# Value products in groups of four, two and two head pairs; the first layer's values in the transposes' banks; more time counted for the heads' transfers

## The chip, the cores and the metric

One core of a Trainium2 chip runs the whole program in one launch. The metric is device time in microseconds (us) of one execution. Of the kernel before, three runs took 275.78, 276.76 and 276.71 us (median 276.71). A fourth execution, the profiled one, took 275.99 us, of which 274.2 us lie between its first and its last instruction; the 1.8 us around that span stand in no row.

## What is computed

A small decoder of two layers over 256 tokens of width 1024, all in float32 accuracy:

```
h = x @ w_in;  c_q, c_kv, k_rope, gate = split(h)          # layer A, latent attention
q  = rms_norm(c_q) @ w_uq;   k_nope, v = rms_norm(c_kv) @ w_ukv
s  = (q_nope . k_nope + q_rope . k_rope) * scale, causal;  p = softmax(s);  o = p @ v
x1 = LayerNorm(alpha * x + (o * silu(gate)) @ w_o)
...
k, v = split(x1 @ w_kv);  q, gate = split(x1 @ w_in)       # layer B, 256 tokens are one block
o  = softmax(causal(rope(q) . rope(k)) * scale) @ v
out = LayerNorm(alpha * x1 + (o * silu(gate)) @ w_o)
```

Both layers have 16 heads with values of 64 columns; the kernel treats them as eight pairs.

## The kernel before

**Products.** TensorE (PE) works on float32r operands. Each factor is split into a high part and a rest (`wh`/`wl` for weights, `act_h`/`act_l`, `x_h`/`x_l`, `big_h`/`big_l` for activations), by `split` (line 400 on ScalarE, line 411 or 415 on VectorE or GpSimd), and each product is three passes: high by high, high by rest, rest by high (`passes`). All are recorded by one helper, so they share line 430; transposes have line 444.

**Order.** No engine's order is written by hand. Every operation is recorded as an `Op` with a counted duration, and `Schedule.order` simulates five queues (PE, ACT, DVE, POOL, SP) with these counts, keeps account of buffers, and writes one fixed order for each engine. At run time each engine works through its own list strictly in order and waits on semaphores. A transfer is counted as landed 1300 ns after its share of the DMA queue, plus `late`, which only the first weights had so far (`LATE`).

```
            if e == "sp":
                x = max(t + 1100, dma)
                dma = x + o.size / 330.0
                o.end = dma + 1300 + o.late
```

**PSUM.** Eight banks: two `s` (scores), two `pt` (transposes), one `pv` (value products), three `proj` (everything else); see `PSUM_BUFS`.

**Attention** (`attention`, both layers). For each pair: `scores` on PE, the softmax on DVE and ACT (tile `e`), fill-in products (`fill`: keys, queries and gates of later pairs), then `transp` (three transposes of `e` per head, copied out to tile `pt`). After every second pair `values` multiplies the transposed weights with the value tile `V`: 64 output columns per head, so two heads share the array, side by side. DVE then multiplies each pair's result by its gate `G` (tile `oa`), and `split` makes `big_h` and `big_l`, the operands of the output product. So each layer has four calls of `values`, of two pairs each, all in the one `pv` bank.

**Heads of layer B.** `rope_moba` makes rotated queries and keys in tile `x_h`; `move_heads` brings them into the heads' layout (tiles `kq0`, `kq1` and `x_l`) by 64 transfers on the SP queue.

**Layer A's values** (`token_products("uv", ...)`) fill four banks, two per half of the tokens ("token 0" and "token 1" below, 128 tokens each), all from the three `proj` banks.

**End.** The last `token_products("ob", ...)` multiplies `big_h`/`big_l` with the output weights: token 0 in two `proj` banks, token 1 in two `s` banks (columns 0 to 511, then 512 to 769) and a `proj` bank (768 to 1023). The seventh and eighth weight units lie in `x_h`/`x_l`, so those products read `x_h,big_h`, `x_l,big_h`, `x_h,big_l`; they need the last two pairs' `big` tiles. `finish_b` does token 0's layer norm on DVE (tile `m`); `last_b` does token 1's in pieces; both end in transfers to `out`.

Of the kernel before, what the change touches and what calls it, by code (L numbers as in the profile page):

```python
# [13 lines left out]
P = 128  # L14
D = 1024
S = 256
# [10 lines left out]
GATES_FIRST = 2  # L27
RAW_BUFS = 5
HL_BUFS = 6
G_BUFS = 5  # L30
LAG = 8
PSUM_BUFS = {"s": 2, "pt": 2, "pv": 1, "proj": 3}

# [20 lines left out]
PLAIN = 2  # L54
PIECES = 4
LATE = 2000

LANES = 8


def on(*key):
    return "pool" if key in POOL else "dve"
# [76 lines left out]
def A(x):  # L139
    if isinstance(x, View):  # L140
        return x.ap()
    return x.tile() if isinstance(x, Val) else x
# [225 lines left out]
def trunk(ctx, tc, W0, xtok, W, WO, gq, gkv, lng, lnb, cosa, sina, coska, sinka, cosb, sinb, maskd, identd, out):  # L368
    nc = tc.nc
# [8 lines left out]
    def C(shape, tag, dtype=F32, at=0):  # L378
        return sc.val(cp, shape, dtype, tag, at=at)

    def T(shape, tag, bufs=2, dtype=F32):
        return sc.val(tp, shape, dtype, tag, bufs)

    def bank(tag):
        return sc.val(pp, [P, 512], F32, tag, PSUM_BUFS[tag])
# [5 lines left out]
    def dma(o, i, size, part=False, r=None, late=0):  # L391
        sc.op("sp", 650 if part else 525, lambda: nc.sync.dma_start(A(o), A(i)), [i] if r is None else r, [o], size).late = late

    def act(o, i, n, func=AF.Copy, scale=1.0, bias=0.0, accum=None):
        dur = (n + (61 if is_ps(i) else 112)) / 1.2
        dur += 93 * (accum is not None) + 93 * isinstance(scale, (View, Val)) + 93 * isinstance(bias, (View, Val))

        def go():
            if func is AF.Copy:
                nc.scalar.copy(A(o), A(i))  # L400
            elif accum is None:
                nc.scalar.activation(A(o), A(i), func, bias=A(bias), scale=A(scale))
            else:
                nc.scalar.activation(A(o), A(i), func, bias=A(bias), scale=A(scale), accum_out=A(accum))  # L404

        sc.op("act", dur, go, [i, scale, bias], [o] + ([accum] if accum is not None else []))
# [20 lines left out]
    def mms(calls, o, r, dur):  # L427
        def go():
            for (out_, lt, rh, st, sp_) in calls:
                nc.tensor.matmul(A(out_), A(lt), A(rh), start=st, stop=sp_, skip_group_check=True)  # L430

        sc.op("pe", dur, go, r, o if isinstance(o, list) else [o], k=len(calls))
# [4 lines left out]
    def passes(o, ah, al, bh, bl, start, stop, n, r=None):  # L437
        mms([(o, ah, bh, start, False), (o, ah, bl, False, False), (o, al, bh, False, stop)],
            o, [ah, al, bh, bl], 3 * mm_cost(n))
# [8 lines left out]
    def split(h, l, src, n, scale=None, eng="dve"):  # L448
        if scale is None:
            act(h, src, n)  # L450
            tt(l, src, h.f32(), ALU.subtract, n, eng)
        else:
            act(h, src, n, AF.Identity, scale=scale)
            stt(l, src, scale, h.f32(), ALU.mult, ALU.subtract, n)
# [10 lines left out]
    def load_raw():  # L465
# [3 lines left out]
        if u < 8:  # L469

            for c0, c1 in ((0, 512), (512, 1280)) if u < PLAIN else ((0, 1280),):
                dma(r[:, c0:c1].at(c0), W0[u, :, c0:c1], (c1 - c0) * 512, late=LATE * (u > 0))
            split(xh[:, u, :].at(u), xl[:, u, :].at(u), r[:, 0:S].at(0), S)
# [49 lines left out]
    def wsl(w, c0, c1):  # L523
        h, l, kk, early = w
        if early == "ob":
            if c0 == 512 and c1 == 1024:
                return tuple(t.halves() for t in (h, l))
            c0, c1 = (LAST, WOB) if c0 == 768 else (c0, c1)
            return h[:, c0:c1], l[:, c0:c1]
        key = (kk, c0 // S * S if early else 0)  # L530
        return h[:, c0:c1].at(key + (0,)), l[:, c0:c1].at(key + (1,))
# [30 lines left out]
    def token_products(name, nk, lhs, tags, lag, done, last=None, last_residual=None):  # L562
        banks = [None, None]
        n1 = nk * (3 if last else 1)
        for i in range(max(nk, n1 + lag)):
            for tok in range(2):
                j = i - lag * tok
                if not 0 <= j < (n1 if tok else nk):
                    continue
                if j == 0:  # L570
                    banks[tok] = [bank(t) for t in tags[tok]]
                k = j % nk
                w = weights(name, k)
                parts = ((0, 512), (512, 1024))
                if tok and last:
                    parts = (((0, 512), (512, 770), (768, 1024))[j // nk],)
                for c0, c1 in parts:
                    h, l = wsl(w, c0, c1)
                    ah, al = lhs(k, tok)
                    o = banks[tok][j // nk if tok and last else c0 // 512][:, 0:c1 - c0]  # L580
                    if last and c1 - c0 == 512 and c0:
                        o = o.rearrange("p (a b) -> p a b", b=S)
                    if last and tok and c0 == 768 and k == 0:
                        last_residual(o)
                    passes(o, ah, al, h, l, k == 0 and not (last and tok and c0 == 768), k == nk - 1, c1 - c0)
                if tok and last:
                    if k == nk - 1:
                        last(banks[tok][j // nk], c0, c1 // S * S)
                elif j == nk - 1:
                    done(tok, banks[tok])  # L590
# [11 lines left out]
    for k in range(8):  # L602
        w = weights("g1", k)
        a, b = xs(k)
        for c in range(8):
            o = g1[c // 2][:, (c % 2) * S:(c % 2) * S + S]
            if k < PLAIN and c < 2:
                u, v = first_raws[k][:, S + c * P:S + (c + 1) * P].at(0), first_raws[k][:, 0:S].at(0)
# [67 lines left out]
    def gate(name, j, rhs):  # L676
# [3 lines left out]
        act(t, ps[:, :S], S, AF.Tanh, scale=0.5)  # L680
        g = T([P, S], "G", G_BUFS)
        stt(g, t, 1.0, ps[:, :S], ALU.add, ALU.mult, S)
# [35 lines left out]
    for g in range(2):  # L718
        ps = bank("proj")
# [63 lines left out]
    def transp(es):  # L783
        r = []
        for e in es:
            pt = bank("pt")
            transposes(pt, [(pt[:, i * P:(i + 1) * P], e[:, c0:c0 + P]) for i, c0 in enumerate((S, 0, P))], [e])
            t = T([P, 384], "pt", 6)
            act(t, pt[:, :384], 384)
            r.append(t)  # L790
        return r

    def values(la, ps_, pts, Vt, ogh, ogl):

        ps, calls, used = bank("pv"), [], []
        for j, p in enumerate(ps_):
            for t in range(2):
                for s in range(2):
                    v = Vt[:, t, 2 * p + s, :].at((t, (2 * p + s) // 8))
                    calls.append((ps[64 * s:64 * s + 64, j * S + t * P:j * S + S], v, pts[j][s][:, t * S:S + t * P], t == 0, t == 1))  # L800
                    used += [v, pts[j][s]]
        mms(calls, ps, used, 250 + 642 * len(ps_))
        for j, p in enumerate(ps_):
            oa = T([P, S], "oa")
            tt(oa, ps[:, j * S:(j + 1) * S], Gs.pop(p), ALU.mult, S)
            split(ogh[:, p, :].at(p), ogl[:, p, :].at(p), oa, S, eng=on("og", la, p))

    def value_evac(Vt, banks, tok):
        for hf in range(2):
            src = banks[hf].rearrange("p (a b) -> p a b", b=64)  # L810
            act(Vt[:, tok, 8 * hf:8 * hf + 8, :].at((tok, hf)), src, 512)

    def attention(la, heads, fill, scale, Vt, ogh, ogl):
        done = []
        for i in range(8):
            hd, keys = heads(i)
            es = scores(la, i, hd, keys, scale)
            fill(i)
            if len(done) == 2:
                values(la, (i - 2, i - 1), done, Vt, ogh, ogl)  # L820
                done = []
            done.append(transp(es))
        values(la, (6, 7), done, Vt, ogh, ogl)

    def heads_mla(p):
        b = p % 4
# [6 lines left out]
    ogh, ogl = C([P, 8, S], "big_h", F32R, AT_ACT), C([P, 8, S], "big_l", F32R, AT_ACT)  # L833
    kq_mla(0)
    kq_mla(1)
    V = C([P, 2, H, 64], "V")
# [1 line left out]
    def lhs_kv(k, tok):  # L838
        return tuple(t[:, k, tok * P:(tok + 1) * P].at(k) for t in (ch, cl))

    token_products("uv", 2, lhs_kv, (("proj", "proj"), ("proj", "proj")), 2, lambda tok, bk: value_evac(V, bk, tok))

    def fill_a(step):
        for nm, i in PLAN_A[step]:
# [87 lines left out]
    def move_heads(step):  # L932
        while moves and moves[0][0] - 3 <= step:
            p, R, base = moves.pop(0)
            hd = HT[p % 3]
            for s in range(2):
                r0 = base + 32 * s
                for v in range(2):
                    dma(hd[32 * v:32 * v + 32, s, 0:3, :].at((s, v, 0)).f32(), R[r0:r0 + 32, v, 1:4, :].at(None).f32(), 98304, True)
                    dma(hd[64 + 32 * v:96 + 32 * v, s, 0:2, :].at((s, v, 1)).f32(), R[r0:r0 + 32, v, 0:4:2, :].at(None).f32(), 65536, True)  # L940

    def heads_moba(p):
        hd = HT[p % 3]
# [33 lines left out]
    def last_residual(o):  # L977
        mms([(o, idr, rh, True, False), (o, idr, rl, False, False)], o, [idr, rh, rl], 2 * mm_cost(S))
# [132 lines left out]
```

## Time and profile before

| | before |
|---|---|
| median of three runs | 276.71 us (275.78 to 276.76) |
| the profiled execution | 275.99 us, its span 274.2 us |
| TensorE busy | 267.3 us, 97% of the span |
| VectorE busy | 217.0 us, 79% |
| ScalarE busy | 164.1 us, 60% |
| GpSimd busy | 44.8 us, 16% |
| granted TensorE clock, mean | 0.997 |

A busy TensorE row is the time in which some product was on its way; products overlap, so two starts stand closer together than one row is long. Start-to-start distances are the price of a product. Times in the rows count from the first instruction of the span.

### The profile page before, as it was taken

How to read it: one execution, taken by the hardware profiler on the slowest of the kernel's cores; microseconds unless marked ns; L12 is line 12 of the kernel's file. 1: busy time of each engine (PE TensorE's matmuls, PEld its weight loads, DVE VectorE, ACT ScalarE, POOL GpSimd, SP SyncE). 2: the span in 40 equal slices, each digit the busy share in tenths (PEclk: the TensorE clock that was granted, in tenths of full speed). 3: DMA queues.
4: the chain of work that ended last, by engine and by line, in shares of the span. 5: the costliest groups of instructions: out<-in, count | busy, mean ns of one | idle time of the engine just before them, and what ended most of it. 6: DMA issues, size and time to landing. Idle time of an engine off the chain costs nothing.

```text
span 274.2 us, 5384 instructions
## 1 busy us (share of the span) xinstructions
PE 267.3 (97%) x1950; PEld 246.3 (90%) x1950; DVE 217.0 (79%) x494; ACT 164.1 (60%) x366; POOL 44.8 (16%) x46
## 2 busy tenths in 40 slices
PE   8999999999999999999999999999999999999991
PEld 6999999999899988878888899999999999887890
DVE  3776889999998789947997436879978998897584
ACT  4864977477774779914372543637856859986000
POOL 3000162300020021111010000602324214021000
PEclk9999999999999999999999999999999999999998
DMA  7999484777334442470459574466759768440022
GB/s 232 405 400 412 164 278 183 238 266 274 115 118 149 158 155 78 138 247 0 148 175 295 203 255 154 155 187 195 273 128 331 200 220 322 117 127 4 0 78 77
DMA packets 18683, 52.46 MB, mean 191 GB/s; under 512 B 2912, under 2 KB 6112, under 8 KB 18656
## 3 DMA queue, kind: packets, MB, share of 16 engines
q1 hardware_dynamic: 18656, 52.12, 56.4%
q8 instruction: 15, 0.25, 0.4%
q14 instruction: 12, 0.10, 0.1%
HBM read 45.81 MB, written 1.05 MB: 171 GB/s over the span
## 4 chain that ended last, share of the span: by engine, by line
PE 93%; issue 3%; DVE 2%; POOL 0%; POOLq 0%; DVEq 0%
PE proj L430 61%; PE s L430 15%; PE pv L430 8%; PE pt L444 5%; PE pt L430 4%; DVE bst L864 1%; DVE m L415 0%; DVE act_h L415 0%; POOL mv L411 0%; POOLq L1107 0%; DVEq L1107 0%; DVE mv L865 0%; DVE mv L422 0%
## 5 line engine op out<-in xcount | busy, mean ns | idle before, releaser
L411 DVE TENSOR_TENSOR wl<-raw,wh 128x1024 fp32r<-128x1024 f32 (+3 forms) x80 | 85.6, 1090 | 21.3 <-ACT wh L400 21.0
L400 ACT CAST wh<-raw 128x1024 fp32r<-128x1024 f32 (+4 forms) x81 | 73.5, 925 | 36.6 <-PE proj L430 17.8
L430 PE MATMUL proj<-act_h,wh 128*128 128x256 f32 x280 | 79.6, 284 | 0.0
L430 PE MATMUL proj<-act_l,wh 128*128 128x256 f32 x280 | 78.5, 280 | 0.0
L430 PE MATMUL proj<-act_h,wl 128*128 128x256 f32 x280 | 78.5, 280 | 0.0
L430 PEld LDWEIGHTS proj<-act_h,wh 128*128 128x128 f32 x280 | 52.8, 188 | 0.0
L430 PEld LDWEIGHTS proj<-act_l,wh 128*128 128x128 f32 x280 | 52.7, 188 | 0.0
L430 PEld LDWEIGHTS proj<-act_h,wl 128*128 128x128 f32 x280 | 52.7, 188 | 0.0
L404 ACT ACTIVATE e<-e,st 128x256 f32<-128x256 f32 x64 | 28.5, 449 | 6.3 <-DVE st L770 6.2
L411 POOL TENSOR_TENSOR big_l<-oa,big_h 128x256 fp32r<-128x256 f32 x14 | 10.8, 786 | 87.7 <-ACT big_h L400 87.7
L430 PE MATMUL s<-kq 128*128 128x256 f32 (+1 forms) x100 | 19.1, 318 | 0.0
L424 DVE TENSOR_SCALAR e<-e,st 128x256 f32<-128x256 f32 x64 | 18.0, 325 | 0.9
L430 PE MATMUL proj<-x_h,wh 128*128 128x256 f32 x64 | 18.5, 289 | 0.0
L430 PE MATMUL proj<-x_h,wl 128*128 128x256 f32 x64 | 18.0, 281 | 0.0
L430 PE MATMUL proj<-x_l,wh 128*128 128x256 f32 x64 | 18.0, 281 | 0.0
L430 PEld LDWEIGHTS s<-kq 128*128 128x128 f32 x100 | 15.6, 190 | 1.6 <-issue 0.3
L400 ACT COPY pt<-pt 128x384 f32<-128x384 f32 x32 | 14.8, 477 | 1.5 <-PE pt L444 1.3
L411 DVE TENSOR_TENSOR x_l<-raw,x_h 128x256 fp32r<-128x256 f32 (+2 forms) x14 | 10.7, 770 | 5.9 <-ACT x_h L400 5.9
L444 PE MATMUL pt<-ident,e 128*128 128x128 f32 x96 | 15.0, 275 | 0.1
L400 ACT CAST x_h<-raw 128x256 fp32r<-128x256 f32 (+2 forms) x14 | 9.4, 685 | 8.7 <-PE s L430 4.3
L411 POOL TENSOR_TENSOR t<-t,t512b 128x512 f32<-128x512 f32 x5 | 6.8, 1364 | 39.0 <-DVE t L411 21.4
L444 PEld LDWEIGHTS pt<-ident,e 128*128 128x128 f32 x96 | 11.0, 140 | 1.4 <-issue 0.7
(190 smaller groups left out, 570.6 us busy)
## 6 DMA issues: line engine op xcount, KB each, us to landing
raw<-in_W SPq DMA_DIRECT2D x58, 512.0 KB, 4.4
raw<-in_WO SPq DMA_DIRECT2D x8, 528.0 KB, 5.4
raw<-in_W SPq DMA_DIRECT2D x6, 640.0 KB, 6.9
raw<-in_W SPq DMA_DIRECT2D x6, 384.0 KB, 5.9
kq<-x_h SPq DMA_DIRECT2D x24, 96.0 KB, 2.2
kq<-x_h SPq DMA_DIRECT2D x24, 64.0 KB, 2.1
m<-in_xtok SPq DMA_DIRECT2D x2, 512.0 KB, 6.4
lng<-in_lng SPq DMA_DIRECT2D x2, 512.0 KB, 3.6
```

The lines of the kernel that those rows point to most:

```text
L400: nc.scalar.copy(A(o), A(i))
L404: nc.scalar.activation(A(o), A(i), func, bias=A(bias), scale=A(scale), accum_out=A(accum))
L411: sc.op(eng, dur, lambda: e.tensor_tensor(A(o), A(a), A(b), op=op), [a, b], [o], lock=not (is_ps(a) or is_ps(b)))
L424: fn = lambda: e.tensor_scalar(A(o), A(a), A(s1), s2, op0=op0, op1=op1)
L430: nc.tensor.matmul(A(out_), A(lt), A(rh), start=st, stop=sp_, skip_group_check=True)
L444: nc.tensor.transpose(A(x), A(y), A(ident))
L864: sc.op("dve", 600, lambda hf=hf, cs=cs: nc.vector.bn_stats(A(st[:, hf, :]), A(z[:, cs])), [z.at(hf)], [st.at(hf)])
```

## The change

Five edits, one of which (the scratch size, line 1104 of the kernel before) makes room in SBUF for the larger buffers.

- `values` takes up to four pairs; the third and fourth pair go into a second bank, from `proj`. `attention` calls it at pair 4 (pairs 0 to 3), pair 6 (4 and 5) and at the end (6 and 7): three calls a layer. Buffers `G` grow from 5 to 7, `pt` tiles from 6 to 10. The call's counted duration becomes 370 ns plus 642 ns a pair (250 before).
- Layer A's values for token 1 go into the two `pt` banks.
- Each of the 64 transfers of layer B's heads is counted as landing 2000 ns later than before.
- The DMA scratch shrinks to 4096 bytes a partition.

```
-G_BUFS = 5
+G_BUFS = 7
+GROUPS = (4, 6)
+MOVE_LATE = 2000
...
-            t = T([P, 384], "pt", 6)
+            t = T([P, 384], "pt", 10)
...
-        ps, calls, used = bank("pv"), [], []
-        for j, p in enumerate(ps_):
+        banks, calls, used = [bank(t) for t in ("pv", "proj")[:(len(ps_) + 1) // 2]], [], []
+        for i, p in enumerate(ps_):
+            ps, j = banks[i // 2], i % 2
...
-        mms(calls, ps, used, 250 + 642 * len(ps_))
+        mms(calls, banks, used, 370 + 642 * len(ps_))
...
-            if len(done) == 2:
-                values(la, (i - 2, i - 1), done, Vt, ogh, ogl)
+            if i in GROUPS:
+                values(la, range(i - len(done), i), done, Vt, ogh, ogl)
...
-        values(la, (6, 7), done, Vt, ogh, ogl)
+        values(la, range(8 - len(done), 8), done, Vt, ogh, ogl)
...
-    token_products("uv", 2, lhs_kv, (("proj", "proj"), ("proj", "proj")), 2, lambda tok, bk: value_evac(V, bk, tok))
+    token_products("uv", 2, lhs_kv, (("proj", "proj"), ("pt", "pt")), 2, lambda tok, bk: value_evac(V, bk, tok))
...
-                    dma(hd[32 * v:32 * v + 32, s, 0:3, :].at((s, v, 0)).f32(), R[r0:r0 + 32, v, 1:4, :].at(None).f32(), 98304, True)
+                    dma(hd[32 * v:32 * v + 32, s, 0:3, :].at((s, v, 0)).f32(), R[r0:r0 + 32, v, 1:4, :].at(None).f32(), 98304, True, late=MOVE_LATE)
...
-    nc = bacc.Bacc("TRN2", target_bir_lowering=False, num_devices=1)
+    nc = bacc.Bacc("TRN2", target_bir_lowering=False, num_devices=1, dynamic_dma_scratch_size=4096)
```

Since the counts and the groups feed the scheduler, the written orders change in many places. Three of them follow; line 430 of the kernel before is line 434 of the change, and 415 is 419.

PE, layer B, the first value products (`V`) of the kernel before, then those of the change; `pt<-ident,e` are transposes, `s<-` scores.

```order
L430 MATMUL pv<-pt,V 64x256 x2
L430 MATMUL pv<-pt,V 64x128 x2
L430 MATMUL pv<-pt,V 64x256 x2
L430 MATMUL pv<-pt,V 64x128 x2
L444 MATMUL pt<-ident,e 128x128 x3
L430 MATMUL s<-kq_1883 128x256 x2
```

```order
L434 MATMUL s<-kq_1891 128x256 x3
L434 MATMUL pv<-pt,V 64x256 x2
L434 MATMUL pv<-pt,V 64x128 x2
L434 MATMUL pv<-pt,V 64x256 x2
L434 MATMUL pv<-pt,V 64x128 x2
L434 MATMUL proj<-pt,V 64x256 x2
L434 MATMUL proj<-pt,V 64x128 x2
L434 MATMUL proj<-pt,V 64x256 x2
L434 MATMUL proj<-pt,V 64x128 x2
L448 MATMUL pt<-ident,e 128x128 x3
```

Two calls have become one of twice the length, its second half in a `proj` bank; the same stands in layer A.

PE, the end: the last products of token 0 (`proj<-x_h`, `proj<-x_l`) and what follows them, before and in the change. `s<-` are token 1's products.

```order
L430 MATMUL proj<-x_h,big_h 128x512
L430 MATMUL proj<-x_l,big_h 128x512
L430 MATMUL proj<-x_h,big_l 128x512
L430 MATMUL s<-wh,big_h 128x512
L430 MATMUL s<-wl,big_h 128x512
L430 MATMUL s<-wh,big_l 128x512
```

```order
L434 MATMUL proj<-x_h,big_h 128x512
L434 MATMUL proj<-x_l,big_h 128x512
L434 MATMUL proj<-x_h,big_l 128x512
L434 MATMUL s<-x_h,big_h 128x512
L434 MATMUL s<-x_l,big_h 128x512
L434 MATMUL s<-x_h,big_l 128x512
```

Before, 15 products of 512 columns and 15 of 258 columns on the other weight units (`wh`, `wl`) still follow token 0's last one, beside all of those shown as `s<-x_h`; in the change these 30 stand ahead of token 0's last ones. The last call of `values` has moved with them: it stands after 15 of token 1's products, where before it stood ahead of all of them.

DVE, the end: token 0's layer norm (tile `m_293` before, `m_292` in the change) and token 1's (`m_320`); `lng` and `lnb` are the layer norm's factors and offsets.

```order
L864 BN_STATS bst<-m_293 128x6
L865 BN_AGGR mv<-bst 128x2
L422 TENSOR_SCALAR mv<-mv 128x1
L415 SCALAR_TENSOR_TENSOR m_293<-m_293,mv,lng 128x512 x2
L415 SCALAR_TENSOR_TENSOR m_293<-m_293,mv,lnb 128x512 x2
L415 SCALAR_TENSOR_TENSOR m_320<-m_320,s 128x512
```

```order
L419 SCALAR_TENSOR_TENSOR m_292<-m_292,mv,lng 128x512
L419 SCALAR_TENSOR_TENSOR m_320<-m_320,s 128x512
L419 SCALAR_TENSOR_TENSOR ms<-s,ms 128x1
L1002 BN_STATS bst_3397<-m_320 128x6
L419 SCALAR_TENSOR_TENSOR m_292<-m_292,mv,lng 128x512
L419 SCALAR_TENSOR_TENSOR m_292<-m_292,mv,lnb 128x512 x2
```

The instructions are the same ones; in the change token 1's first pieces are interleaved with token 0's, and all of token 0's still stand ahead of token 1's closing statistics (`BN_STATS` of the `proj` bank).

## Rows read from the trace of the kernel before

**Rows 1.** Page, part 1: busy us (share of the span) x instructions.

```profile
PE 267.3 (97%) x1950; PEld 246.3 (90%) x1950; DVE 217.0 (79%) x494; ACT 164.1 (60%) x366; POOL 44.8 (16%) x46
```

**Rows 2.** Waits, PE alone: line waited for, us in total, times, longest.

```profile
PE pv L430 <- PEq L1104: 0.8, 1, 0.8
```

**Rows 3.** Timeline of PE, layer A: start us, us, what (two stretches).

```profile
76.45 0.28 PE L430 MATMUL proj<-act_l,wh 128*128 128x256 f32 x1
76.56 0.28 PE L430 MATMUL proj<-act_h,wl 128*128 128x256 f32 x1
76.90 0.52 PE L444 MATMUL pt<-ident,e 128*128 128x128 f32 x3
...
104.87 0.28 PE L430 MATMUL proj<-x_h,wl 128*128 128x256 f32 x1
105.11 0.67 PE L430 MATMUL s<-kq 128*128 128x256 f32 x2
```

**Rows 4.** Timeline of PE, the end, from token 0's last products.

```profile
254.34 0.40 PE L430 MATMUL proj<-x_h,big_h 128*128 128x512 f32 x1
...
257.14 0.39 PE L430 MATMUL s<-wh,big_h 128*128 128x512 f32 x1
...
262.00 0.28 PE L430 MATMUL s<-wh,big_h 128*128 128x258 f32 x1
...
264.91 0.40 PE L430 MATMUL proj<-act_l 128*128 128x256 f32 x2
...
267.88 0.27 PE L430 MATMUL proj<-x_h,big_l 128*128 128x256 f32 x1
```

**Rows 5.** Timeline of DVE, the end.

```profile
256.63 0.69 DVE L415 SCALAR_TENSOR_TENSOR m<-m,proj 128x512 f32<-128x512 f32 x1 [3.04 <-PE proj L430]
...
262.36 0.68 DVE L415 SCALAR_TENSOR_TENSOR m<-m,s 128x512 f32<-128x512 f32 x1
...
263.74 0.14 DVE L422 TENSOR_SCALAR bst<-bst 128x1 f32<-128x1 f32 x1
265.11 0.42 DVE L415 SCALAR_TENSOR_TENSOR m<-m,s 128x256 f32<-128x256 f32 x1 [1.23 <-PE s L430]
...
266.49 1.27 DVE L415 SCALAR_TENSOR_TENSOR act_h<-m,ms,lng 128x256 f32<-128x256 f32 x3
268.19 0.43 DVE L996 BATCH_NORM_STATS2 bst<-proj 128x6 f32<-128x256 f32 x1 [0.42 <-PE proj L430]
```

**Rows 6.** Timeline of PE around layer B's last value products.

```profile
249.45 0.39 PE L430 MATMUL proj<-wl,big_h 128*128 128x512 f32 x1
249.68 0.39 PE L430 MATMUL proj<-wh,big_l 128*128 128x512 f32 x1
250.00 1.52 PE L430 MATMUL pv<-pt,V 128*64 128x256 f32 x16
251.45 0.50 PE L430 MATMUL proj<-wh,big_h 128*128 128x512 f32 x1
251.79 0.40 PE L430 MATMUL proj<-wl,big_h 128*128 128x512 f32 x1
```

**Rows 7.** Chain that ended last, in order of time: start us, us, what.

```profile
30.67 26.24 PE proj L430 x200
...
72.22 1.31 PE s L430 x8
```

**Rows 8.** DMA view: queues with packets, MB and share; issues with KB and us to landing.

```profile
q1 hardware_dynamic: 18656, 52.12, 56.4%
...
kq<-x_h SPq DMA_DIRECT2D x24, 96.0 KB, 2.2
kq<-x_h SPq DMA_DIRECT2D x24, 64.0 KB, 2.1
```

**Rows 9.** Windows: stretch, length, then busy us (x instructions) of PE, PEld, DVE, ACT, POOL.

```profile
256.63:268.15 11.52, 11.52 (x74) 10.30 (x72) 9.63 (x22) 0.00 (x0) 0.99 (x1) 1.00 0.12 46
```

**Rows 10.** Timeline of DVE and POOL after layer B's last value products.

```profile
251.64 0.76 DVE L411 TENSOR_TENSOR oa<-pv,G 128x256 f32<-128x256 f32 x2
252.58 0.73 POOL L411 TENSOR_TENSOR big_l<-oa,big_h 128x256 fp32r<-128x256 f32 x1 [10.21 <-ACT big_h L400]
252.87 0.72 DVE L411 TENSOR_TENSOR big_l<-oa,big_h 128x256 fp32r<-128x256 f32 x1 [0.47 <-ACT big_h L400]
```

**Rows 11.** Page, part 5: group, count, busy us, mean ns, idle before.

```profile
L411 DVE TENSOR_TENSOR wl<-raw,wh 128x1024 fp32r<-128x1024 f32 (+3 forms) x80 | 85.6, 1090 | 21.3 <-ACT wh L400 21.0
```

More of the change, by code (lines that the diff above doesn't have):

```diff
@@ L799, in values @@
                     v = Vt[:, t, 2 * p + s, :].at((t, (2 * p + s) // 8))
-                    calls.append((ps[64 * s:64 * s + 64, j * S + t * P:j * S + S], v, pts[j][s][:, t * S:S + t * P], t == 0, t == 1))
-                    used += [v, pts[j][s]]
-        mms(calls, ps, used, 250 + 642 * len(ps_))
-        for j, p in enumerate(ps_):
+                    calls.append((ps[64 * s:64 * s + 64, j * S + t * P:j * S + S], v, pts[i][s][:, t * S:S + t * P], t == 0, t == 1))
+                    used += [v, pts[i][s]]
+        mms(calls, banks, used, 370 + 642 * len(ps_))
+        for i, p in enumerate(ps_):
+            ps, j = banks[i // 2], i % 2
             oa = T([P, S], "oa")
@@ L938, in move_heads @@
                 for v in range(2):
-                    dma(hd[32 * v:32 * v + 32, s, 0:3, :].at((s, v, 0)).f32(), R[r0:r0 + 32, v, 1:4, :].at(None).f32(), 98304, True)
-                    dma(hd[64 + 32 * v:96 + 32 * v, s, 0:2, :].at((s, v, 1)).f32(), R[r0:r0 + 32, v, 0:4:2, :].at(None).f32(), 65536, True)
+                    dma(hd[32 * v:32 * v + 32, s, 0:3, :].at((s, v, 0)).f32(), R[r0:r0 + 32, v, 1:4, :].at(None).f32(), 98304, True, late=MOVE_LATE)
+                    dma(hd[64 + 32 * v:96 + 32 * v, s, 0:2, :].at((s, v, 1)).f32(), R[r0:r0 + 32, v, 0:4:2, :].at(None).f32(), 65536, True, late=MOVE_LATE)
     def heads_moba(p):
```

## The prediction

> **What bounds the kernel now.** I read the engine shares first: TensorE is busy for 97% of the span, the next engine for 79% [rows 1]. A busy share could hide waits, so the waits of TensorE alone come second: one, 0.8 us, at the very start [rows 2]. Third, the start-to-start distances of TensorE after the first microseconds: I found two hesitations. One transpose starts 0.34 us after the product ahead of it, where its neighbours stand 0.11 us apart; one score starts after 0.24 us instead of about 0.12 [rows 3]. They are worth 0.23 and 0.12 us, 0.35 us together. So from its start to its last product at 268.15 us (267.88 + 0.27, [rows 4]) TensorE is one unbroken list, and a faster or slower neighbour changes nothing unless TensorE waits for it. Last I read the end: the closing statistics on VectorE start at 268.19, 0.04 us after the last product, and VectorE sat idle for 0.42 us ahead of them [rows 5]. After that start 6.0 us follow (274.2 - 268.19), in which nothing of the change lies. So the time is: the length of TensorE's list, plus what VectorE still has to do when the list ends.
>
> **Part 1: fewer value calls.** Around one call, the start of the last 512-column product ahead (249.68) and that of the second one behind (251.79) lie 2.11 us apart [rows 6]. Two 512-column intervals are 2 x 0.233 = 0.47 us (twelve products from 254.34 to 257.14, [rows 4]). The call's own columns are those of a pair of score calls, which take 1.31 us at full width [rows 7]; here two heads run side by side at half width, so I take 1.31 again, as an estimate. 2.11 - 0.47 - 1.31 leaves 0.33 us for entering and leaving. What shows directly is less: 0.09 us ahead (0.32 instead of 0.23) and 0.11 us behind (0.34 instead of 0.23), 0.20 us. The change has two calls fewer, one in each layer: 0.40 to 0.66 us saved. I take 0.66, since the account of the columns has to close. No row shows a step from one bank to another inside a call; it lies between 0 and another 0.33 us for each of the two long calls, and I take 0, since both banks are written by products of one shape.
>
> The Trainium skill, "TensorEngine Tiling (Array Packing)", section "Tiling Modes", says that changing the mode, not just the tile, drains TensorE; by it the step from bank to bank costs nothing, and the +3.0 us reached below stand; were each step priced like a mode change, the sum would be +3.7 us.
>
> **Part 2: the hesitations.** The two of [rows 3] may go or stay, since their places are rearranged: 0 to 0.35 us saved. I take 0.1 us.
>
> **Part 3: the first layer's values in the transposes' banks.** The stretch that holds them, 26.24 us with 200 records, is one unbroken piece of TensorE in the chain [rows 7]. A bank that comes free sooner frees nobody. Zero, hidden by TensorE's own products; if that cover were gone, the bank's copy would show, but the change gives more banks there, not fewer.
>
> **Part 4: buffers and scratch.** Larger buffers can only let the scheduler move things; the moves are counted where they land. For the smaller scratch: all data moves through the hardware queue, 52.12 MB of it [rows 8], and none through a software one. Zero.
>
> **Part 5: the heads' transfers, 2 us more each.** This is a count in the scheduler, not work. The chip lands them 2.1 to 2.2 us after issue [rows 8], and no product waits for one [rows 2], so there is no wait to remove. What the count does is move the scores of layer B's heads later in TensorE's list, hence the softmax, the transposes and the last value call. The order shows where that ends: the last call now stands behind 15 of token 1's products, and token 0's last twelve stand 30 products nearer to the end. Those 30 are 15 of 512 and 15 of 258 columns. 15 x 0.233 = 3.50 us. The 258-column interval is 0.121 us (24 products from 262.00 to 264.91, [rows 4]); 15 x 0.121 = 1.82 us. So **token 0 is finished 5.32 us later, measured back from TensorE's end**.
>
> VectorE pays for it. Before, it began token 0's layer norm at 256.63 and had until 268.19, that is 11.56 us, of which it was idle 1.23 and 0.42 us [rows 5]: 9.91 us of work in a row, 22 instructions, 9.63 us of it busy time [rows 9]. The same 22 instructions stand ahead of the closing statistics in the change, and the engine takes them in order. They now have 11.56 - 5.32 = 6.24 us until TensorE ends. 9.91 - 6.24 = **3.67 us late**. Nothing else runs then: TensorE has finished, and what waits behind VectorE is the closing statistics, the last five normalising steps and the transfers out, all of it on the path. Interleaving token 1's pieces into token 0's changes no instruction. The bounds: 3.4 us if the busy 9.63 us alone count, 3.9 us if a few more short gaps between dependent instructions appear.
>
> Do token 0's last twelve products wait? They need the last two pairs' rests. Before, these were ready 1.79 us (GpSimd, 252.58 + 0.73) and 2.07 us (VectorE, 252.87 + 0.72) after the value products ended (250.00 + 1.52) [rows 6, 10]. In the change 3 products of 512 and 15 of 258 columns stand between: 0.70 + 1.82 = 2.52 us, and the first rest is read only by the third of the twelve. Zero, unless VectorE is over half a microsecond behind.
>
> **The sum.** -0.66 (calls) - 0.1 (hesitations) + 3.67 (end) = +2.9 us. The scores and transposes are reshuffled throughout layer B, and one or two new hesitations of the size of [rows 3] are likely: +0.1 us, which makes +3.0. On the profiled execution, 275.99 us: 279.0. The three other runs have a median 0.72 us above it; on that, 279.7. I take the mean of the four, 276.3, as the base: **279.3 us**. About 0.5% (1.4 us) is what a measurement of this kernel can tell from no change; +3.0 is 1.1%.
>
> **The rivals.**
> - *TensorE gets new waits on top.* The long call holds a `proj` bank that key, query and gate products want, until VectorE has multiplied two more pairs by their gates: two such steps took 0.76 us [rows 10], and a weight rest of 1.1 us on average [rows 11] can stand ahead of them. Also the last head's softmax now has 15 products of 512 columns between its scores and its transposes, 3.5 us. For it: VectorE is 79% busy [rows 1]. Against it: two `proj` banks remain, and the hesitations of before are tenths. Price: 0.5 to 0.8 us at each of two or three places, 1 to 2 us in all: 280.3 to 281.3 us. Chance 0.17. The Trainium skill's "TensorEngine Tiling (Array Packing)", section "Performance Considerations", warns in the same direction that packing speeds up TensorE but not the emptying of PSUM; by it these waits would be likelier than I hold them, while the rows have two pairs' products at 1.45 us against 0.76 us of emptying.
> - *The end stays hidden, and the gain remains* (the other side). Place: VectorE's 22 instructions between token 0's last product and TensorE's end. If they fit, the saved 0.66 us and the 0.35 us of hesitations are all that is left: 276.3 - 1.0 = 275.3 us. It decides at 6.24 us of cover: they would have to run 1.6 times as fast, or token 0 would have to finish 3.7 us sooner. For it: only that VectorE's rows might be stretched by a neighbour before. Against it: in that stretch ScalarE does nothing and GpSimd one instruction [rows 9], so nothing stretched them. Chance 0.04.
> - *The body gains more than I count.* The 1.31 us for a call's columns is my estimate, not a row. If the half-width columns take less, entering and leaving take more: at 1.0 us a call the two calls saved give 2.0 us instead of 0.66, and the sum is 276.3 + 1.6 = 277.9 us. For it: a call's own row cannot be split. Against it: 0.20 us is all that shows outside it [rows 6]. Chance 0.07.
>
> **How the numbers follow.** The forecast proper (279.3, give or take 1 us for the base and the bounds above) has 0.72. The range runs from 278.0 to 281.3: it takes in the forecast and the first rival, and leaves out the two others and the tails. Faster by over 0.5%: 0.03, the second rival. Within 0.5% (up to 278.1): 0.08, the rest of it and the lower part of the third. Slower: 0.89.
>
> **What would show it.** In the changed profile: TensorE's last product about 0.5 to 0.7 us earlier in the span; six stretches of value products instead of eight, two of them with 32 records; VectorE without idle time from token 0's last product to the closing statistics, which then start 3.5 to 4 us after TensorE's end instead of 0.04; a span near 277.3 us. The forecast is wrong if VectorE shows idle time ahead of the closing statistics, or if TensorE's waits add up to over 1 us.

## The result and the profile after

The changed kernel takes 278.65 us (median of 6 runs, 278.11 to 279.62), the kernel before, run beside it, 276.08 us (275.33 to 276.76): ratio 1.0085, 95% interval 1.0059 to 1.0110. That is 2.6 us slower; forecast were 3.0. Medians and ratios from here on leave out executions over 1.5% above the fastest of their kernel: three of twelve with 500 counted (278.49 to 280.68 us), two of the kernel before (279.41 and 279.45), and one of the changed kernel with held transfers (442.28 us at a mean granted clock of 0.558, for a reason that stays open). The profiled execution of the changed kernel has a span of 276.7 us and took 278.5 us, against 274.2 and 275.99.

Engine shares and the waits of TensorE, from the page and the view of waits (columns as in [rows 1, 2]):

```profile
PE 265.5 (96%) x1950; PEld 245.1 (89%) x1950; DVE 220.1 (80%) x494; ACT 164.3 (59%) x366; POOL 44.4 (16%) x46
```

```profile
PE pv L434 <- PEq L1110: 0.8, 1, 0.8
PE s L434 <- DVE st L774: 0.5, 1, 0.5
PE s L434 <- ACT wh L404: 0.2, 1, 0.2
```

TensorE is as full as before; half a microsecond of waiting for VectorE is new, and so are 0.2 us for ScalarE in the first microseconds. By the letter a sign of being wrong has come ("TensorE's waits add up to over 1 us": they are 1.5 us here, of which 0.8 stood there before); only 0.7 us of it is new.

The mean granted clock fell from 0.997 to 0.987, which could pass for a cause of 1%. It is none. The windows (stretch, length, busy us of PE, PEld, DVE, ACT, POOL, granted clock, DMA share, GB/s) show full speed (1.00, 2.4 GHz) while TensorE works and the lower level only behind its end; the kernel before has 1.00 from 28 to 268 us as well.

```profile
28.00:268.00 240.00, 238.62 (x1748) 219.96 (x1746) 197.52 (x445) 146.75 (x332) 41.79 (x39) 1.00 0.53 173
267.17:276.69 9.52, 0.00 (x1) 0.00 (x0) 6.05 (x17) 0.00 (x0) 0.55 (x1) 0.63 0.29 110
```

The time went elsewhere. TensorE's last product, from the timeline of PE (start us, us, engine, line, operation, out<-in, count), answers to the last of [rows 4]:

```profile
266.90 0.27 PE L434 MATMUL proj<-x_h,big_l 128*128 128x256 f32 x1
```

and VectorE's rows of the end, from its timeline, to [rows 5]:

```profile
260.94 0.69 DVE L419 SCALAR_TENSOR_TENSOR m<-m,proj 128x512 f32<-128x512 f32 x1 [2.75 <-PE proj L434]
...
264.02 0.74 DVE L419 SCALAR_TENSOR_TENSOR m<-m,mv,lng 128x512 f32<-128x512 f32 x1
264.68 0.68 DVE L419 SCALAR_TENSOR_TENSOR m<-m,s 128x512 f32<-128x512 f32 x1
...
265.74 0.73 DVE L419 SCALAR_TENSOR_TENSOR m<-m,mv,lng 128x512 f32<-128x512 f32 x1
266.39 1.41 DVE L419 SCALAR_TENSOR_TENSOR m<-m,mv,lnb 128x512 f32<-128x512 f32 x2
267.72 0.42 DVE L1002 BATCH_NORM_STATS2 bst<-m 128x6 f32<-128x256 f32 x1
...
269.48 1.27 DVE L419 SCALAR_TENSOR_TENSOR act_h<-m,ms,lng 128x256 f32<-128x256 f32 x3
270.67 0.42 DVE L1002 BATCH_NORM_STATS2 bst<-proj 128x6 f32<-128x256 f32 x1
```

TensorE ends at 267.17, 0.98 us earlier than before. VectorE starts token 0's layer norm at 260.94 and works without a bracket (no idle time that the view marks) to the closing statistics at 270.67, 9.73 us. So these start 3.50 us after TensorE's end, where before it was 0.04: +3.46 - 0.98 = +2.48 us, the growth of the span.

The calls. Around the first call with four pairs, from the timeline of PE of the changed kernel:

```profile
94.33 0.28 PE L434 MATMUL proj<-act_h,wl 128*128 128x256 f32 x1
94.53 1.52 PE L434 MATMUL pv<-pt,V 128*64 128x256 f32 x16
95.88 1.47 PE L434 MATMUL proj<-pt,V 128*64 128x256 f32 x16
97.28 0.88 PE L448 MATMUL pt<-ident,e 128*128 128x128 f32 x6
```

and around a call with two, of the kernel before:

```profile
226.88 0.28 PE L430 MATMUL proj<-act_h,wl 128*128 128x256 f32 x1
227.08 1.52 PE L430 MATMUL pv<-pt,V 128*64 128x256 f32 x16
228.53 0.88 PE L444 MATMUL pt<-ident,e 128*128 128x128 f32 x6
```

From the product ahead to the one behind, four pairs take 97.28 - 94.33 = 2.95 us and two take 1.65. Two calls of two would be 3.30, of which 0.12 is one more ordinary interval of 256-column products: 3.30 - 0.12 - 2.95 = 0.23 us. This stops at the first transpose behind, and the second is late as well. The view of PE from 97.63 on starts with it:

```profile
97.45 0.49 PE L448 MATMUL pt<-ident,e 128*128 128x128 f32 x3
```

It stands 0.17 us behind the first (97.28), where its followers stand 0.11 us apart, and in the kernel before it is the same (228.70 behind 228.53). So a call saved between such neighbours is worth 0.29 us. Among 512-column products the second one behind is late by 0.10 us [rows 6], and behind layer A's first call, which stood between scores, the second score is too. From the single starts in the two traces, the eight calls of before cost 2.52 us beyond their columns and the ordinary intervals beside them, the six of the change 1.89: 0.63 us saved. The columns are those of the prediction's estimate: a pair in the second bank takes 0.65 us (95.88, 96.53, 97.19 without the way out), two pairs 1.30. The two records at the step from bank to bank stand 0.10 us apart, as inside a bank: the step has no price of its own. The Trainium skill, "TensorEngine Tiling (Array Packing)", section "Tiling Modes", says that changing the tiling mode, not just the tile, drains TensorE. The trace agrees: 0.20 to 0.35 us for each time into the 128*64 tiles and out again, nothing for the step between banks inside.

The new hesitation, from the timeline of PE, and what VectorE did then:

```profile
72.95 0.28 PE L434 MATMUL proj<-act_h,wl 128*128 128x256 f32 x1
73.78 1.11 PE L434 MATMUL s<-kq 128*128 128x256 f32 x5 [0.55 <-DVE st L774]
```

```profile
69.76 2.35 DVE L415 TENSOR_TENSOR wl<-raw,wh 128x1024 fp32r<-128x1024 f32 x2
72.14 0.70 DVE L749 COPY kq<-proj 64x512 f32<-64x512 f32 x1
72.86 0.48 DVE L774 CUSTOM_DVE_ANT_0 e<-s,masks,sca 128x256 f32<-128x256 f32 x1
73.27 0.08 DVE L774 DVE_READ_ACCUMULATOR2_ANT st<- 128x1 f32 x1
...
73.54 0.09 DVE L774 DVE_READ_ACCUMULATOR2_ANT st<- 128x1 f32 x1
```

A score starts 0.83 us after the product ahead instead of 0.12: the bank it needs is emptied by a softmax step that stands on VectorE behind two weight rests and a key copy. The last row shown is the one that releases it. That is +0.71 us. The rival had named such weight rests ahead on VectorE, but for a `proj` bank held by a long call; here it is an `s` bank, and the first long call comes only at 94.53. Before, a call of `values` stood between the scores at this place (73.46). That its going brings the wait is not shown, though none of the five profiled executions without a call of four has it, and eight of the nine with one do.

### The profile page after: what moved, and what is told of

Read it like the earlier page. It is cut to its first block, busy times and chain, and to the rows that moved or that the text cites. A ratio compares the mean times of both kernels' runs of the same rounds, so it can differ in the third digit from the quotient of the medians.

```text
span 276.7 us, 5391 instructions
## 1 busy us (share of the span) xinstructions
PE 265.5 (96%) x1950; PEld 245.1 (89%) x1950; DVE 220.1 (80%) x494; ACT 164.3 (59%) x366; POOL 44.4 (16%) x46
## 4 chain that ended last, share of the span: by engine, by line
PE 92%; issue 3%; DVE 2%; DMA 1%; POOL 0%; POOLq 0%; ACT 0%; DVEq 0%; SPq 0%
PE proj L434 60%; PE s L434 16%; PE pv L434 6%; PE pt L434 5%; PE pt L448 5%; DMA raw<-in_W 1%; DVE bst L870 1%; DVE m L419 0%; DVE act_h L419 0%; POOL mv L415 0%; POOLq L1113 0%; ACT wh L404 0%; DVEq L1113 0%; SPq L396 0%; DVE e L774 0%
## 5 line engine op out<-in xcount | busy, mean ns | idle before, releaser
L415 DVE TENSOR_TENSOR wl<-raw,wh 128x1024 fp32r<-128x1024 f32 (+3 forms) x80 | 87.5, 1115 | 22.3 <-ACT wh L404 21.9
L415 POOL TENSOR_TENSOR big_l<-oa,big_h 128x256 fp32r<-128x256 f32 x14 | 10.2, 741 | 91.3 <-ACT big_h L404 91.2
L428 DVE TENSOR_SCALAR e<-e,st 128x256 f32<-128x256 f32 x64 | 18.7, 335 | 0.9
L415 POOL TENSOR_TENSOR x_h<-t,x_h 128x512 fp32r<-128x512 f32 x7 | 11.2, 1618 | 13.5 <-DMA raw<-in_W 11.8
L415 POOL TENSOR_TENSOR t<-t,t512b 128x512 f32<-128x512 f32 x5 | 7.7, 1553 | 33.3 <-DVE t L415 19.3
```

The lines of the kernel that those rows point to most:

```text
L415: sc.op(eng, dur, lambda: e.tensor_tensor(A(o), A(a), A(b), op=op), [a, b], [o], lock=not (is_ps(a) or is_ps(b)))
L428: fn = lambda: e.tensor_scalar(A(o), A(a), A(s1), s2, op0=op0, op1=op1)
```

## The experiments

Twelve runs, each beside runs of the kernel before on the same chip. In all of them I read two things: when VectorE starts token 0's layer norm and when TensorE ends (the cover), and how late the closing statistics are.

**The count alone, and its opposite.** The changed kernel without the count:

```
-MOVE_LATE = 2000
+MOVE_LATE = 0
```

> The changed kernel with the added lateness of the heads' transfers set back to 0; groups, banks, buffers and scratch stay. Theory 'end' (the 2 us per transfer push token 0's last products to the end of TensorE's list, and VectorE is then 3.5 us late): token 0's last product again has the cover of before (24 products of 512 and 24 of 258 columns follow it), the closing statistics start within 0.1 us of TensorE's end, and only the two value calls saved remain: 0.3 to 1.0 us below the kernel before, 275.1 to 275.8 us. Theory 'groups' (the long calls hold a bank and TensorE waits): as slow as the changed kernel, 278 us or more.

276.84 us, ratio 1.0017 (0.9988 to 1.0047). The end is hidden again, as expected:

```profile
269.14 0.43 DVE L1002 BATCH_NORM_STATS2 bst<-proj 128x6 f32<-128x256 f32 x1 [0.42 <-PE proj L434]
```

TensorE ended at 269.10, so 0.04 us. But the gain of the calls is not there: the waits of TensorE are

```profile
PE s L434 <- DVE st L774: 0.5, 1, 0.5
PE s L434 <- DVE e L428: 0.4, 1, 0.4
```

and I missed the time by about 1 us. The kernel before with nothing but the count:

```
-dma(hd[...], R[...], 98304, True)
+dma(hd[...], R[...], 98304, True, late=2000)
...
-dma(hd[...], R[...], 65536, True)
+dma(hd[...], R[...], 65536, True, late=2000)
```

> The kernel before with the 2 us per transfer alone; pairs, banks and buffers as before. Theory 'end': 6 products of 512, 15 of 258 and 26 of 256 columns follow token 0's last one, six of 258 columns (0.73 us) more than in the changed kernel, so the closing statistics start 2.7 us after TensorE's end (3.46 - 0.73); TensorE's end as before; time 276.1 + 2.7 = 278.8 us. Theory 'groups': the time of before, 276.1 us.

279.61 us, ratio 1.0119 (1.0087 to 1.0151). Closing statistics at 271.73, TensorE's end at 268.98: 2.75 us. The rest is a wait in layer B's body, which the changed kernel does not have:

```profile
PE pt L444 <- DVE e L424: 1.5, 1, 1.5
```

The count with calls of two pairs, all else as changed:

```
-GROUPS = (4, 6)
+GROUPS = (2, 4, 6)
```

> The changed kernel with pairs again instead of groups of four (four calls a layer), the lateness kept. Theory 'end': 12 products of 258 columns (1.46 us) more than in the changed kernel follow token 0's last one, so the closing statistics start 2.0 us after TensorE's end and the time is 276.1 + 2.0 = 278.1 us. Theory 'groups': the time of before, 276.1 us.

278.57 us, ratio 1.0077 (1.0047 to 1.0107). Late by 271.36 - 269.31 = 2.05 us, with the same wait of 1.5 us. So the count brings the slow end, with or without the other parts of the change. With a quarter of it (MOVE_LATE = 500):

> The changed kernel with a lateness of 500 ns instead of 2000. Theory 'end': the order has the cover of before behind token 0's last product (24 of 512, 24 of 258 columns), so the closing statistics start within 0.1 us of TensorE's end; the two value calls saved remain, 275.0 to 275.6 us. If the lateness costs in proportion to its size, a quarter of the changed kernel's loss remains: 276.5 us or more.

275.60 us, ratio 0.9985 (0.9950 to 1.0020): no loss and no sure gain. The end is hidden (closing statistics at 271.41, TensorE's end at 271.38), so the cost is not in proportion to the count. In the profiled execution, 279.22 us, TensorE waited 1.9 us for a head's transfer, until 236.66, and then had half the clock (0.50, 1.2 GHz) for 3.4 us, in which 256-column products started 0.21 us apart instead of 0.12:

```profile
237.97:241.38 3.41, 3.41 (x18) 2.81 (x18) 1.73 (x11) 2.84 (x9) 0.00 (x0) 0.50 0.32 78
```

This is the only profile here in which the clock fell ahead of TensorE's end; the wait of 2.3 us shown further down left it at 1.00.

**VectorE's queue, lightened.** In both kernels the last four normalising steps of token 0 are left out:

```
+        if light:
+            return
         for hf, cs in enumerate(cols):
             stt(z[:, cs].at(hf), z[:, cs].at(hf), mv[:, 0:1].at(0), gb[:, cs], ...
...
-        layer_norm(bk, x1[tok], x1[tok], gb, bb)
+        layer_norm(bk, x1[tok], x1[tok], gb, bb, light=True)
```

> The changed kernel, with token 0's last four normalising steps of layer B left out (token 0's output is then not normalised). TensorE's list is the same. In the changed kernel these four take 2.64 us of VectorE's queue (264.02 to 264.68, 265.74 to 267.72). Theory, VectorE's queue at the end sets the time: the closing statistics start 3.50 - 2.64 = 0.86 us after TensorE's last product, and the time falls by 2.6 us, to about 276.0. Rival, the time was lost in TensorE's list or in the transfers out, and VectorE only fills the time: no change, 278.7.

275.46 us, ratio 0.9962 (0.9938 to 0.9987), against 1.0085 with them. TensorE's list and end are the same to 0.04 us (267.21), and the closing statistics came forward to

```profile
267.91 0.42 DVE L1004 BATCH_NORM_STATS2 bst<-proj 128x6 f32<-128x256 f32 x1
```

0.70 us late instead of 3.50: 2.80 us less for four steps that stand at 2.64 us in the queue, and the span fell by the same 2.8 (276.7 to 273.9).

> The kernel before, with the same four steps left out (token 0's output is then not normalised). Theory: they lie beside TensorE's products, so the closing statistics still start 0.04 us after the last product, the idle time ahead of them grows from 0.42 us to at least 2 us, and the time stays at 276.1. Rival, VectorE's work at the end is on the path in both kernels: about 273.5.

276.75 us, ratio 1.000 (0.997 to 1.003). Its VectorE had idle stretches of 2.54 and 1.39 us instead of token 0's steps, and nothing was gained. The two runs together show that the same four instructions are free in one kernel and on the path in the other. This run had a second use. Its TensorE list is that of the kernel before, instruction for instruction, as are those of the other engines up to token 0's last layer norm, and its waits are

```profile
PE pt L444 <- ACT e L404: 1.1, 1, 1.1
PE pv L430 <- PEq L1106: 0.8, 1, 0.8
PE s L430 <- DMA kq<-x_h: 0.4, 1, 0.4
```

One execution of this list had no such wait in its body [rows 2], another 1.5 us of them, 0.4 for a head's transfer.

**How much count is too much.** With 1000:

> The changed kernel with 1 us more counted instead of 2. Counted in the order, 12 of 512 columns and 15 of 258 that the change took from behind token 0's last products are back; 3 of 512 fewer stand there than before, 0.7 us of cover, while VectorE had 1.65 us idle to lose. Theory, the end decides: closing statistics within 0.1 us of the last product, and the value calls' 0.66 us as the gain: 275.4 to 276.2, the upper part if one or two waits of TensorE come back, as with 0 counted. Rival, any lateness costs: between 276.8 and 278.7.

275.11 us, ratio 0.9955 (0.9929 to 0.9982): faster than the kernel before, and 1.3% faster than the changed one. VectorE starts token 0 at 255.88, TensorE ends at 266.71, the closing statistics follow at once, with idle time ahead of them:

```profile
266.75 0.43 DVE L1002 BATCH_NORM_STATS2 bst<-proj 128x6 f32<-128x256 f32 x1 [0.42 <-PE proj L434]
```

Its only waits after the start are the one of 0.5 us in layer A. The 2 us for the first three pairs only:

```
-..., True, late=MOVE_LATE)
+..., True, late=MOVE_LATE * (p < 3))
```

> The changed kernel with the 2 us counted for the first three pairs of heads only (p < 3), nothing for the others. The same 0.7 us less cover behind token 0 than before, so by theory the end stays hidden: closing statistics within 0.1 us of the last product; 275.4 to 276.2. If the 2 us served to keep TensorE from waiting for late transfers or late softmaxes (the rival, by which 0 and 500 counted lost their gain again), waits of 0.5 to 2 us show in layer B's later heads, 276.5 or more.

276.90 us, ratio 1.0015 (0.9983 to 1.0047). The end is hidden (270.32, TensorE ends at 270.28), but the rival was right on the body. TensorE's row:

```profile
239.22 0.59 PE L434 MATMUL s<-kq 128*128 128x256 f32 x3 [2.31 <-DMA kq<-x_h]
```

and the view of the heads' tile from 222 to 246 us:

```profile
L396 SPq DMA_DIRECT2D kq<-x_h x16: 559/598/606, 230.8 to 243.5; - x16
...
DMA to landing us min/median/max: 2.0/2.2/7.8
```

A transfer that lands in 2.2 us as a rule took up to 7.8 here, and the score waited for it. The windows of this run, from 228 us (stretch, length, busy us of PE, PEld, DVE, ACT, POOL, granted clock, DMA share, GB/s), show with what it competed:

```profile
228.00:231.00 3.00, 3.00 (x29) 2.83 (x26) 3.00 (x6) 2.61 (x8) 2.75 (x2) 1.00 0.97 353
231.00:234.00 3.00, 3.00 (x28) 3.00 (x27) 2.36 (x13) 3.00 (x12) 2.51 (x4) 1.00 1.02 365
```

The DMA engines are full, with the 528 KB weights of the output product. The Trainium skill, "DMA: Bandwidth & Descriptors", section "Queues, rings and completion order", says that each DMA engine consumes descriptors in ring order; by that a small transfer issued behind the weights on the same queue stands behind their bytes. The landings agree. In this run the last of these weights, issued at 229.05, landed after 9.2 us, at 238.26, and the four transfers that the score needs, issued from 230.76, landed at 238.56, 238.72, 238.91 and 239.08. It is so everywhere: in the 14 traces a heads' transfer (or one of the four extra ones below) is the first behind a run of weights in layer B 56 times, and each time it landed 0.2 to 1.1 us after the last of these weights, which landed 2.1 to 7.7 us after its issue. No run here took the weights out of the way.

With 1400:

> The changed kernel with 1.4 us counted instead of 2. Behind token 0's last products stand 6 products of 512 columns fewer than before, 1.4 us less cover: 11.56 - 1.4 = 10.2 us for the 9.7 to 9.9 us of work that VectorE needs. Theory: just hidden, closing statistics at most 0.3 us behind the last product, time as with 1 us counted, 275.0 to 275.8. Rival, VectorE's pieces of token 1 do not fit into the gaps and 0.5 to 1 us shows at the end: 276 to 276.5.

276.62 us, ratio 1.0010 (0.9981 to 1.0039). At the end the theory held to the edge: cover 10.13 us, closing statistics 0.04 us late and no idle time ahead of them. The time missed, for the wait of the first experiments is back:

```profile
PE pt L448 <- DVE e L428: 1.4, 1, 1.4
```

**Room for the transfers.** Four small transfers into an unused buffer stand in SyncE's queue ahead of pair 6's, not counted by the scheduler:

```
+    def hold(o, i, size, part, late=0):
+        def go():
+            for q in range(4):
+                nc.sync.dma_start(A(held[0:32, q, :]), A(i[:, 0, 0:64]))
+            nc.sync.dma_start(A(o), A(i))
...
-                    dma(hd[32 * v:32 * v + 32, s, 0:3, :] ...
+                    (hold if (p, s, v) == (6, 0, 0) else dma)(hd[32 * v:32 * v + 32, s, 0:3, :] ...
```

> The kernel before, with four small transfers into an unused buffer put into SyncE's queue ahead of pair 6's first transfer, not counted by the scheduler, so that every other order stays. At 0.6 us each they hold the transfers of the last two pairs back by 2.4 us. In the kernel before, pair 6's first transfer is issued at 230.43 and its first score starts at 235.31, 4.9 us; the first head's four transfers take 4 x 0.6 us to issue and some 2.1 us to land, 4.5 us. Theory, in the kernel before TensorE is only tenths of a microsecond behind these transfers: a wait of about 2.0 us for them, time 278.1 to 278.7. Rival, the transfers have room (the trace of before shows no wait for them): under 0.5 us.

> The changed kernel with the same four transfers ahead of pair 6's. Here 8.4 us lie between pair 6's first transfer (231.22) and its first score (239.59), 3.9 us more than landing needs. Theory, this room is what the counted 2 us bought: no wait for the transfers, 278.6 as without. Rival, late transfers delay this list as they delay the other: 280.5 or more.

> The kernel with 1 us counted and the same four transfers ahead of pair 6's. 7.5 us lie between pair 6's first transfer (227.54) and its first score (235.02), 3.0 us more than landing needs, so by theory no wait or tenths: 275.1 to 275.7. Rival, with half the counted time half of the delay shows: 276.3 or more.

The kernel before with it: 277.17 us, ratio 1.0030 (0.9996 to 1.0064). The four went out from 228.28, into time in which SyncE had been idle, so pair 6 was held back by less than the 2.4 us that I had written. Pair 6's first transfer and its first score:

```profile
230.85 0.52 SPq L938 DMA_DIRECT2D kq<-x_h  x1
```

```profile
236.36 0.59 PE L430 MATMUL s<-kq 128*128 128x256 f32 x3 [1.43 <-DMA kq<-x_h]
```

This run is 0.44 us ahead at layer B's start, so the delay is 230.85 - (230.43 - 0.44) = 0.86 us, and the wait 1.4 us. The delay alone does not make this wait: the last of the four transfers that the score needs landed 0.95 us ahead of it in the kernel before. Here it was issued 1.0 us later and took 3.3 us to land instead of 2.0. The changed kernel with it: 278.46 us, ratio 1.0081 (1.0048 to 1.0114), as without. Here the delay is larger, 233.81 against 231.22 + 0.87 (this run is 0.87 us later than the changed kernel's at layer B's start), 1.7 us, and TensorE's list of waits holds no transfer:

```profile
PE pv L434 <- PEq L1120: 0.8, 1, 0.8
PE s L434 <- DVE st L774: 0.5, 1, 0.5
```

With 1000 counted: 275.92 us, ratio 0.9971 (0.9945 to 0.9996), 1.2 us of delay, waits of 0.2 for a transfer and 0.2 for a softmax; between what the two theories said. The waits (1.4, 0.2 and 0 us) have the order of the room between transfer and score (4.9, 7.5 and 8.4 us). But the three were not pushed alike: the landing that the score needs came 2.3, 2.7 and 0.8 us later than without the four, so the changed kernel's zero says less than it seems to. By the times the first and the third run alone decide nothing: the first's interval touches 1, the third's overlaps that without the four.

## Why the prediction was right, step by step

**The end (+3.67, measured +3.46).** This was the step that decided. VectorE's work and the cover, over the runs (first normalising step of token 0, TensorE's end, closing statistics, us):

```
kernel              first step   TensorE ends   cover   closing   late
before                  256.63         268.15   11.52    268.19   0.04
without the count       256.89         269.10   12.21    269.14   0.04
1000 counted            255.88         266.71   10.83    266.75   0.04
1400 counted            258.86         268.99   10.13    269.03   0.04
count, pairs            261.63         269.31    7.68    271.36   2.05
before with count       262.00         268.98    6.98    271.73   2.75
changed                 260.94         267.17    6.23    270.67   3.50
```

The cover of the changed kernel is 6.23 us; 6.24 was worked out from the 30 products. In the last three rows cover and lateness add up to 9.73 us each time, the length of VectorE's work when it runs without a pause; the forecast had 9.91 by subtracting the two long idle times, and the shorter pauses went too. As soon as the cover is above this length, nothing shows. The rival by which the end stays hidden is excluded.

**The calls (-0.66, measured -0.63).** The account of the columns closed: 1.30 us for a call's own columns against the estimated 1.31, and 0.29 to 0.35 us for entering and leaving where the two calls went. The 0.20 us that "shows directly" was too little: 0.05 us more stand between the call's first products (94.53 to 94.80 is 0.26 us, where the second bank has 0.21), and 0.10 us between its last product and the first one behind. The rival of a much larger gain rested on a call's row that "cannot be split"; narrower views split it, and exclude the rival. No price for the second bank: right.

**Hesitations (-0.1 and +0.1, measured +0.30).** This is what is left of the stretch from layer A's first score to TensorE's end, 211.07 us against 211.40, when 0.63 is taken off for the calls. In it are the +0.71 at 72.95 and the 0.22 that went at 76.56 [rows 3]; the other one of [rows 3] stands in the changed kernel too (a score 0.24 us behind the product at 104.34). The other, smaller ones I did not trace one by one. This is the term of the sum that was mis-sized: one new wait was larger than "the size of [rows 3]". Waits on top came at this one place; 280.3 us was not reached.

**The start (not in the sum, measured -0.65).** TensorE passed layer A's first score 0.65 us earlier than before. The runs of this study had the same point anywhere from 1.08 us earlier to 0.20 later, the kernel before with the count alone 0.63 earlier, the changed kernel's own list, held, 0.20 later: it varies from execution to execution, and I put it down to no edit.

3.46 - 0.63 + 0.30 - 0.65 = 2.48, the growth of the span. By the two profiled executions, roughly, the forecast of 279.3 was above 278.65 by this start, by 0.2 us at the end, and by a base of 276.3 where the runs beside it had 276.08, less 0.3 us by which the hesitations were larger. That it came so near is in part luck: the start belongs to no edit, and the sum was built on an execution of the kernel before without a wait in its body, which others of the same list have.

**What failed** is a sentence beside the sum: "no product waits for one [rows 2], so there is no wait to remove". It held for one execution. The landing that I read there was a median, 2.1 to 2.2 us [rows 8]; the kernel before, too, had heads' transfers that took up to 5.8 us, and up to 7.9 in the lightened run. Layer B's length, from its first key or query product to the last product of all, tells what the count does for TensorE (us):

```
list of the kernel before      108.31   110.46 (lightened)   109.80 (held)
list of the changed kernel     107.89   107.90 (lightened)   107.89 (held)
1000 counted                   107.86   109.49 (held)
1400 counted                   109.52
500 counted                    111.50 (3.4 us of it at half the clock)
without the count              109.31
count, pairs                   109.89
before with count              109.83
2 us for the first three       110.78
```

The changed list comes out the same three times, the one of before does not. The count buys room between a head's transfers and its scores: pair 6's last needed transfer had landed 0.95 us ahead of its score in the kernel before, 2.2 us with 1000 counted and 2.3 in the changed kernel, but 0.1 to 0.3 without the count, with 500 and with 2 us for the first three. It is paid at the end, where token 0 comes late. With 1000 enough of both is left. Room is not all of it: the three lists with 1400 counted, or with the whole count and calls of two, had over 3 us of it and lost 1.4 to 1.5 us to a softmax. That the best count is 1000 is not shown: 500 and 1400, each side of it, gave no sure gain, and the wait for a softmax comes and goes with the order. What would remove it was not tried.

## What to carry to other kernels

A kernel whose TensorE is full has its time decided at the end of its list: count what each other engine still has to do after the last input that it gets early, and how many products cover it, before a scheduler's costs are changed. A cost that the scheduler counts for a transfer is a margin; it is worth what late landings cost in the runs, not in one profile, so look at the longest landing, at what was issued ahead of it on the same queue, and at the room between a landing and its reader, not at the median and at one list of waits. And a term that is sure (a few dropped switches) is easily smaller than what moving the same work does to the last ten microseconds.

## What was not expected of the hardware

Small transfers between buffers of the same core, 64 to 96 KB, landed in 2.0 to 2.2 us as a rule, and in up to 7.9 us (before, lightened), 7.8 (with 2 us for the first three pairs), 5.8 (before) and 5.5 us (changed), all in layer B and behind weights in SyncE's queue, with whose landing theirs came; in the run of the 7.8 us the DMA engines' share was 0.97 to 1.02 in the six microseconds around its issue. And two executions of one and the same TensorE list differed by 2 us in layer B, 108.31 and 110.46, at the same granted clock (1.00 up to TensorE's end in both).
